# Feed-forward input product of a two-layer encoder as seven 2x2 block products

## Chip, cores, metric

The kernel runs on one core of one Trainium2 chip, in one launch. The metric is the time of an execution on the device in microseconds; the time before is the median of three runs.

## What is computed

Two encoder layers over 512 tokens of width 1024, all in float32. Each layer has a mixer (latent attention and a convolution), a cross attention to 256 memory tokens and a SwiGLU feed-forward part, each with a residual and a layer norm. The change touches the feed-forward part, with FFN_HIDDEN = 2816:

```python
def swiglu_ffn(x, w_in, w_down):
    gu = x @ w_in
    g, up = gu[..., :FFN_HIDDEN], gu[..., FFN_HIDDEN:]
    return (jax.nn.silu(g) * up) @ w_down
...
y = memory_cross_attention(x, mem, xa_w_q[l], xa_w_kv[l], xa_w_o[l])
x = layer_norm(ALPHA * x + y, ln2_g[l], ln2_b[l])
y = swiglu_ffn(x, ffn_w_in[l], ffn_w_down[l])
x = layer_norm(ALPHA * x + y, ln3_g[l], ln3_b[l])
```

## The kernel before

Every float32 operand of a matrix product is split into a rounded high part and a residue; `mm3` (L248) makes a product of three matmuls: high x high, high x residue, residue x high. ACT casts the high part, and the residue is a subtraction on DVE or Pool, or, in `added_weights` (L282), ACT writes the negated high part and an accumulating DMA from Pool's queue adds the weights from memory.

Tokens are four tiles `t` of 128. For the feed-forward input the normed x is transposed by TensorE (`transpose_x`, L426) into `xT`, eight parts of 128 features x 512 tokens, each as high part and residue. The 2816 gate and 2816 up features make 22 tiles `j` each. `ffn_blocks` (L1092) makes 44 `Block`s (L481), gate and up in turn; a block is a weight tile of 128 x 1024, fetched over SP's queue into one of three `raw` buffers, and split into one of seven `whi` and `wlo` buffers (RING); blocks from the fourth on use `added_weights`. `Block.done` runs 8 x 3 matmuls of 512 columns into one PSUM bank (`accb`, four of them; `psb` gives four more in turn). After a gate block, ACT takes tanh and DVE one operation, and after an up block DVE one more, which writes the hidden tile `hid`. Then the down projection runs over the 22 hidden tiles with weights `fdn`, and `tail` adds the residual x, which has stayed in its buffers, and norms.

Ahead of it stands the tail of the cross attention (`tail`, L513): for each token tile `second_half(t)` (L1083) makes 24 matmuls of 512 columns, and `Norm` (L457) does the residual and norm on DVE with two small Pool operations (L450, L454). The transposes of tile t-2 follow. Behind the last, `blocks[0].first`, `blocks[1].first` and `blocks[2].first` run 24 matmuls each on the first 256 tokens while tiles 2 and 3 are normed and transposed.

The order on the engines is a scheduler's, by priority and readiness, except in stretches under `issue_order` (L158): there each engine named gets its instructions in the order of the program. In the kernel before, the mixer and the start stand under it; the cross attention's tail and `ffn` do not. All engines work their queues in order. Big tiles (26 of 4 KB a partition, `bigt`) and scratch tiles (nine of 544 floats, `scr`) are shared by all stages.

## Time and profile before

| | us |
|---|---|
| runs before: median (lowest to highest) of 3 | 1485.58 (1484.5 to 1486.39) |
| the profiled execution's own time | 1483.78 |
| its span, first to last instruction | 1481.9 |
| TensorE busy in the span | 1450.8 (98%) |
| ACT busy | 721.9 (49%) |
| DVE busy | 704.1 (48%) |
| Pool busy | 469.0 (32%) |

All times of the trace are of the profiled execution, counted from its first instruction. An operation's length in the timeline includes its way through the engine's pipeline; operations that follow each other start closer together than their lengths say, so costs are read from start to start, matmuls included. A DMA's landing is counted from its issue. Layer 0's feed-forward input runs from 379 to 623 us, layer 1's from 1110 to 1354.

### The profile page before, as it was taken

The page shows a single profiled execution, that of the slowest core. Times are in us where ns is not written, and L with a number is a line of the kernel's source. Part 1 is how long each engine was busy: PE and PEld are TensorE (multiplying, and loading weights), DVE is VectorE, ACT ScalarE, POOL GpSimd, SP SyncE. Part 2 cuts the span into 40 slices and gives each one's busy share as a digit, 9 for nine tenths or more (in the row PEclk, how much of TensorE's full clock was granted, in tenths as well). Part 3 has the DMA queues.
Part 4 walks back from the last instruction along what each step waited for, and adds up shares of the span by engine and source line. Part 5 has one row for each costly group of instructions (what it writes and reads, how often), then busy time and mean ns, then how long its engine had stood idle before and what let it go on. Part 6 is the DMA issues. An engine that isn't in the chain of part 4 may idle for free.

```text
span 1481.9 us, 21183 instructions
## 1 busy us (share of the span) xinstructions
PE 1450.8 (98%) x8159; PEld 1255.3 (85%) x8159; DVE 704.1 (48%) x1187; ACT 721.9 (49%) x1278; POOL 469.0 (32%) x665
## 2 busy tenths in 40 slices
PE   8899999999999999999999999999999999999997
PEld 8799988988988888888889998888889888888886
DVE  7999677565411111310569986685662111114005
ACT  3677772452544444543146777624525444446330
POOL 2789762000211111211157987410012111111111
PEclk9999999999999999999999999999999999999999
DMA  5434343351798999999333434423419989899971
GB/s 181 149 94 150 113 157 107 100 158 56 179 212 194 197 189 194 227 195 198 113 103 122 143 122 122 157 80 105 147 57 235 194 195 197 188 194 218 197 140 57
DMA packets 64452, 227.27 MB, mean 153 GB/s; under 512 B 7328, under 2 KB 7360, under 8 KB 64352
## 3 DMA queue, kind: packets, MB, share of 16 engines
q1 hardware_dynamic: 43616, 150.75, 31.6%
q0 software_dynamic: 20736, 75.17, 28.9%
q8 instruction: 64, 1.05, 0.3%
q14 instruction: 36, 0.29, 0.1%
HBM read 213.31 MB, written 8.39 MB: 150 GB/s over the span
## 4 chain that ended last, share of the span: by engine, by line
PE 75%; DVE 10%; DMA 5%; ACT 5%; POOL 3%; issue 2%; SPq 0%; POOLq 0%; DVEq 0%; ACTq 0%
PE accb L250 19%; PE accb L251 18%; PE accb L252 18%; PE psb L250 5%; PE psb L251 5%; PE psb L252 5%; DMA raw<-in_xo 3%; DVE convb L632 2%; DVE wlo L226 2%; DVE p L862 1%; DMA raw<-in_xq 1%; ACT whi L225 1%; PE convb L250 1%; PE convb L252 1%; PE convb L251 1%
## 5 line engine op out<-in xcount | busy, mean ns | idle before, releaser
L250 PE MATMUL accb<-xTh,whi 128*128 128x512 f32 (+1 forms) x1104 | 400.0, 364 | 1.6 <-ACT whi L225 1.3
L251 PE MATMUL accb<-xTl,whi 128*128 128x512 f32 (+1 forms) x1104 | 400.7, 364 | 0.5 <-DVE xTl L436 0.4
L252 PE MATMUL accb<-xTh,wlo 128*128 128x512 f32 (+1 forms) x1104 | 399.7, 363 | 0.4 <-DVE wlo L226 0.4
L287 ACT CAST whi<-raw 128x1024 fp32r<-128x1024 f32 x126 | 132.7, 1055 | 339.4 <-PE accb L251 255.6
L250 PEld LDWEIGHTS accb<-xTh,whi 128*128 128x128 f32 x1104 | 208.3, 190 | 35.7 <-ACT xTh L433 2.7
L251 PEld LDWEIGHTS accb<-xTl,whi 128*128 128x128 f32 x1104 | 209.4, 190 | 33.2 <-DVE xTl L436 1.7
L252 PEld LDWEIGHTS accb<-xTh,wlo 128*128 128x128 f32 x1104 | 209.5, 190 | 32.5 <-DVE wlo L226 0.6
L289 POOL DMA_DIRECT2D wlo<-in_fin x82 | 71.0, 866 | 345.8 <-ACT wlo L288 336.0
L322 POOL TENSOR_TENSOR wlo<-raw,whi 128x1024 fp32r<-128x1024 f32 (+1 forms) x63 | 152.1, 2416 | 58.7 <-ACT whi L314 58.7
L1102 DVE SCALAR_TENSOR_TENSOR scr<-scr,accb 128x512 f32<-128x512 f32 x44 | 30.3, 688 | 253.3 <-ACT scr L1101 253.3
L632 DVE SCALAR_TENSOR_TENSOR convb<-ch,hvec,convb 128x511 f32<-128x511 f32 (+9 forms) x180 | 132.5, 736 | 5.6 <-ACT convb L629 1.7
L288 ACT ACTIVATE wlo<-whi 128x1024 fp32r<-128x1024 f32 x126 | 133.2, 1057 | 2.2
L226 DVE TENSOR_TENSOR wlo<-raw,whi 128x1024 fp32r<-128x1024 f32 (+1 forms) x49 | 56.6, 1158 | 128.2 <-ACT whi L225 127.4
L450 POOL TENSOR_SCALAR ve<-mv 128x1 f32<-128x1 f32 x32 | 27.5, 860 | 244.2 <-DVE mv L471 235.4
L289 POOL DMA_DIRECT2D wlo<-in_fdn x44 | 38.0, 863 | 198.4 <-ACT wlo L288 193.1
L1104 DVE SCALAR_TENSOR_TENSOR hid<-scr,accb 128x512 f32<-128x512 f32 x44 | 30.2, 687 | 136.7 <-PE accb L252 136.7
L225 ACT CAST whi<-raw 128x1024 fp32r<-128x1024 f32 (+1 forms) x49 | 48.8, 1002 | 85.9 <-PE accb L252 33.3
L623 POOL TENSOR_TENSOR cs<-cs,scr 128x511 f32<-128x511 f32 (+29 forms) x60 | 73.6, 1226 | 29.5 <-ACT scr L621 28.3
L314 ACT CAST whi<-raw 128x1024 fp32r<-128x1024 f32 (+1 forms) x63 | 66.6, 1059 | 6.0 <-PE accb L252 1.7
L250 PE MATMUL accb<-whi,hs 128*128 128x512 f32 x176 | 68.6, 389 | 0.0
L251 PE MATMUL accb<-wlo,hs 128*128 128x512 f32 x176 | 68.5, 389 | 0.0
L252 PE MATMUL accb<-whi,hs 128*128 128x512 f32 x176 | 68.5, 389 | 0.0
(297 smaller groups left out, 3160.5 us busy)
## 6 DMA issues: line engine op xcount, KB each, us to landing
raw<-in_fin SPq DMA_DIRECT2D x88, 512.0 KB, 3.6
wlo<-in_fin POOLq DMA_DIRECT2D x82, 512.0 KB, 5.9
raw<-in_fdn SPq DMA_DIRECT2D x44, 512.0 KB, 3.6
wlo<-in_fdn POOLq DMA_DIRECT2D x44, 512.0 KB, 6.1
raw<-in_xk SPq DMA_DIRECT2D x16, 512.0 KB, 3.8
raw<-in_xv SPq DMA_DIRECT2D x16, 512.0 KB, 3.6
raw<-in_wo SPq DMA_DIRECT2D x16, 512.0 KB, 3.6
raw<-in_xq SPq DMA_DIRECT2D x16, 512.0 KB, 3.6
```

Of the source, the lines that this page charges most:

```text
L225: nc.scalar.copy(hi, src)
L226: nc.vector.tensor_tensor(lo, src, hi.bitcast(F32), op=ALU.subtract)
L250: nc.tensor.matmul(o, l[0], r[0], start=first, stop=False)
L251: nc.tensor.matmul(o, l[0], r[1], start=False, stop=False)
L252: nc.tensor.matmul(o, l[1], r[0], start=False, stop=last)
L287: nc.scalar.copy(hi[:, :1024], raw[:, :1024])
L288: nc.scalar.activation(lo[:, :1024], hi[:, :1024].bitcast(F32), AF.Copy, scale=-1.0)
L289: nc.gpsimd.dma_start(out=lo[:, :1024], in_=src, accum_op=ALU.add)
L314: nc.scalar.copy(hi, raw)
L322: eng.tensor_tensor(lo, raw, hi.bitcast(F32), op=ALU.subtract)
L623: nc.gpsimd.tensor_tensor(o[:, d:], o[:, d:], part, op=ALU.add)
L632: nc.vector.scalar_tensor_tensor(out=o[:, d:], in0=src[:, :SEQ - d], scalar=tap(m, d), in1=o[:, d:], op0=ALU.mult, op1=ALU.add)
```

## The change

For each feature tile j, gate and up become the two rows of a 2x2 block matrix whose two columns are the halves of the 1024 input features; the tokens become two columns of 256 (tiles 0, 1 and tiles 2, 3). The product of 2x2 by 2x2 blocks is made with seven block products instead of eight, each of 4 x 3 matmuls of 256 columns (`Pair.product`), on seven weight blocks (gate halves "11" and "12", up half "22", sums "s1" to "s4") and seven token parts ("11", "21", "22", "t1" to "t4"), each held as high part and residue (`Halves` has the token parts, two big tiles each). Weight sums are made on DVE from the fetched tiles (`sums`, `sum4`), their high parts on ACT (`hi`), their residues on DVE (`lo`). Gate tiles and the up tile's second half are split on ACT with an accumulating DMA on Pool's queue (`added`, called by `split_gate` and `split_up`). The token differences are made on Pool (`less`), tile by tile, then transposed and split (`put`). The seven products are put together on DVE out of PSUM (`early_sums`, `late_sums`, 5 operations), then tanh on ACT and `hidden`, two operations on DVE.

The tail of the cross attention becomes `tail_pairs`: the loop over token tiles without `issue_order` (in it parts "11" and "21" are made, the gates of tiles 0 and 1 are split, and the sums of tile 0), then the token sums and the first products of tiles 0 to 2 under it. The loop over j in `ffn` stands under `issue_order` as well. The normed x no longer stays in its buffers: each tile is stored to memory (`xm`, on Pool's queue) and loaded again on SP's queue before the down projection.

```diff
+        def put(self, name, src, t):
...
+            pt = psb()
+            for k in range(4):
+                nc.tensor.transpose(pt[:, blk(k)], src[:, blk(k)], ident)
+            hi, lo = (v[:, :, blk(t % 2)] for v in self.parts[name])
+            split(pt.rearrange("p (k c) -> p k c", c=P), hi, lo)
...
+        def sums(self, x, t):
+
+            b11, b21, b12, b22 = (x[i][:, blk(h, 512)] for i in (t, t + 2) for h in range(2))
+
+            def less(a, b):
+                o = scr(name="tsum")[:, :512]
+                nc.gpsimd.tensor_tensor(o, a, b, op=ALU.subtract)
+                return o
+
+            self.put("22", b22, t)
+            yield
+            t1 = less(b12, b11)
+            self.put("t1", t1, t)
+            yield
+            t2 = less(b22, t1)
+            self.put("t2", t2, t)
+            yield
+            self.put("t4", less(b21, t2), t)
+            yield
+            self.put("t3", less(b22, b12), t)
+            yield
...
+        def added(self, hi, lo, raw, src):
+            nc.scalar.copy(hi, raw)
+            nc.scalar.activation(lo, hi.bitcast(F32), AF.Copy, scale=-1.0)
+            nc.gpsimd.dma_start(out=lo, in_=src, accum_op=ALU.add)
...
+        def product(self, o, w, xs_):
+            for k in range(4):
+                mm3(o, cut(self.ops[w], ALL, k, ALL), cut(xs_.parts[PARTNER.get(w, w)], ALL, k, ALL), k == 0, k == 3)
...
+            self.product(self.v[:, 0:256], "11", xs_)
...
+        def copy1(self):
+            self.one = scr(name="one")[:, :512]
+            nc.scalar.copy(self.one[:, 0:256], self.v[:, 0:256])
...
+            self.product(self.v[:, 0:256], "12", xs_)
...
+            self.product(self.v[:, 256:512], "s4", xs_)
...
+            self.product(self.z[:, 256:512], "s2", xs_)
+            self.product(self.z[:, 0:256], "s3", xs_)
...
+            self.product(self.z[:, 0:256], "22", xs_)
+            self.product(self.z[:, 256:512], "s1", xs_)
...
+        def early_sums(self):
+            z, h0, h1 = self.z, slice(0, 256), slice(256, 512)
+            self.u = scr(name="u")[:, :512]
+            nc.vector.tensor_tensor(self.u[:, h0], z[:, h1], self.one[:, h0], op=ALU.add)
+            nc.vector.tensor_tensor(self.u[:, h1], z[:, h0], self.u[:, h0], op=ALU.add)
+
+        def late_sums(self, dst):
+            z, u, h0, h1 = self.z, self.u, slice(0, 256), slice(256, 512)
+            nc.vector.tensor_tensor(self.one[:, h1], z[:, h1], u[:, h0], op=ALU.add)
+            nc.vector.tensor_tensor(dst.rearrange("p (a c) -> p a c", a=2), z.rearrange("p (a c) -> p a c", a=2),
+                                    u[:, h1].rearrange("p (a c) -> p a c", a=1).broadcast_to([P, 2, 256]), op=ALU.add)
+            nc.vector.tensor_tensor(self.v, self.v, self.one, op=ALU.add)
+            self.th = scr()[:, :512]
+            nc.scalar.activation(self.th, self.v, AF.Tanh, scale=0.5)
...
+    PARTNER = {"12": "21", "s4": "22", "22": "t4", "s1": "t1", "s2": "t2", "s3": "t3"}
...
+        with issue_order(tc, ORDERED):
+            early, late = xs_.sums(x, 0), xs_.sums(x, 1)
+            pairs[2].fetch_gate()
+            pairs[0].p1(xs_)
+            pairs[0].copy1()
+            pairs[0].sum4()
+            pairs[1].p1(xs_)
+            pairs[1].copy1()
+            next(early)
+            pairs[2].split_gate()
+            pairs[1].fetch_gate()
+            next(early)
+            pairs[0].p2(xs_)
+            pairs[0].split_up()
+            next(early)
+            pairs[1].fetch_up()
+            pairs[2].fetch_gate()
+            next(early)
+            pairs[1].p2(xs_)
+            next(early)
+            pairs[0].hi("s1", "s4")
+            pairs[0].lo("s1", "s4")
+            pairs[2].p1(xs_)
+            pairs[2].copy1()
+            for _ in range(2):
+                next(late)
+            pairs[2].p2(xs_)
+            for _ in range(3):
+                next(late)
...
+                if "12" in pair.ops:
+                    pair.p2(xs_)
+                if after:
+                    after.split_up()
+                if before:
+                    before.late_sums(dst(j - 1))
+                pair.p67(xs_)
+                if after:
+                    after.sums()
+                    after.hi("s3", "s2")
+                if before:
+                    before.hidden(dst(j - 1))
+                pair.early_sums()
+                if after:
+                    after.sum4()
+                    after.hi("s1")
+                    after.lo("s3", "s2")
+                pair.p3(xs_)
+                if j + 2 < NJ:
+                    pairs[j + 2].fetch_up()
+                if j + 3 < NJ:
+                    pairs[j + 3].fetch_gate()
+                if 3 <= j + 2 < NJ:
+                    pairs[j + 2].split_gate()
+                if after:
+                    after.lo("s1")
+                    if after.v is None:
+                        after.p1(xs_)
+                    after.hi("s4")
+                    after.lo("s4")
+                    if j + 1 >= 3:
+                        after.copy1()
+                pair.p45(xs_)
...
+        x = load_x(xm)
```

## Rows read from the trace of the kernel before

**Rows 1.** The page's busy time and share of the span of each engine:

```profile
PE 1450.8 (98%) x8159; PEld 1255.3 (85%) x8159; DVE 704.1 (48%) x1187; ACT 721.9 (49%) x1278; POOL 469.0 (32%) x665
```

**Rows 2.** Windows: stretch, length, each engine's busy us, PEclk, DMA share, GB/s:

```profile
379.46:623.24 243.78, 243.70 (x1153) 204.65 (x1152) 40.97 (x66) 110.15 (x132) 43.08 (x51) 1.00 0.91 203
1109.85:1353.61 243.76, 243.68 (x1154) 204.70 (x1152) 40.97 (x66) 110.13 (x132) 42.57 (x50) 1.00 0.91 203
620.00:640.00 20.00, 20.00 (x90) 16.55 (x89) 13.44 (x22) 16.86 (x27) 3.44 (x4) 1.00 0.94 223
```

**Rows 3.** Timeline, TensorE: start, length, line, out<-in, shape; matmuls 1 and 49:

```profile
479.76 0.39 PE L250 MATMUL accb<-xTh,whi 128*128 128x512 f32 x1
...
490.64 0.39 PE L250 MATMUL accb<-xTh,whi 128*128 128x512 f32 x1
```

**Rows 4.** Timeline, TensorE: eight transposes, then first and last of 66 matmuls:

```profile
379.46 0.60 PE L430 MATMUL psb<-ident,x 128*128 128x128 f32 x4
379.90 0.60 PE L430 MATMUL convb<-ident,x 128*128 128x128 f32 x4
...
382.31 0.28 PE L250 MATMUL accb<-xTh,whi 128*128 128x256 f32 x1
...
390.11 0.28 PE L252 MATMUL accb<-xTh,wlo 128*128 128x256 f32 x1
```

**Rows 5.** List of waits of TensorE: us in total, times, longest:

```profile
PE psb L553 <- DMA mem<-in_mem: 5.0, 1, 5.0
```

**Rows 6.** Timeline, DVE and ACT: runs of like operations end to end:

```profile
381.13 0.76 DVE L436 TENSOR_TENSOR xTl<-psb,xTh 128x256 fp32r<-128x256 f32 x2
...
626.35 3.71 DVE L226 TENSOR_TENSOR hs<-hid,hs 128x512 fp32r<-128x512 f32 x6 [0.78 <-ACT hs L225]
...
623.28 1.05 ACT L287 CAST whi<-raw 128x1024 fp32r<-128x1024 f32 x1
624.23 0.62 ACT L225 CAST hs<-hid 128x512 fp32r<-128x512 f32 x1
...
625.71 3.22 ACT L225 CAST hs<-hid 128x512 fp32r<-128x512 f32 x6
```

**Rows 7.** Page's groups by line, Pool: xcount | busy, mean ns | idle:

```profile
L322 POOL TENSOR_TENSOR wlo<-raw,whi 128x1024 fp32r<-128x1024 f32 (+1 forms) x63 | 152.1, 2416 | 58.7 <-ACT whi L314 58.7
...
L289 POOL DMA_DIRECT2D wlo<-in_fin x82 | 71.0, 866 | 345.8 <-ACT wlo L288 336.0
```

**Rows 8.** Timeline, DVE and Pool: norms of token tiles 2 and 3, layer 0:

```profile
375.55 1.28 DVE L475 SCALAR_TENSOR_TENSOR x<-x,mv,gb 128x1024 f32<-128x1024 f32 x1
...
384.61 1.28 DVE L477 SCALAR_TENSOR_TENSOR x<-x,rstd,gb 128x1024 f32<-128x1024 f32 x1
...
375.60 1.31 POOL L450 TENSOR_SCALAR ve<-mv 128x1 f32<-128x1 f32 x1 [4.01 <-DVE mv L471]
...
382.76 0.22 POOL L450 TENSOR_SCALAR ve<-mv 128x1 f32<-128x1 f32 x1 [1.03 <-DVE mv L471]
```

**Rows 9.** DMA issues in 377:386, 440:600, 614:634: KB, median us to landing:

```profile
wlo<-in_fin POOLq DMA_DIRECT2D x3, 512.0 KB, 9.0
...
wlo<-in_fin POOLq DMA_DIRECT2D x28, 512.0 KB, 5.7
raw<-in_fin SPq DMA_DIRECT2D x24, 512.0 KB, 3.6
...
wlo<-in_fdn POOLq DMA_DIRECT2D x4, 512.0 KB, 7.5
raw<-in_fdn SPq DMA_DIRECT2D x3, 512.0 KB, 5.8
```

**Rows 10.** Windows around TensorE's longest wait, columns as in rows 2:

```profile
49.80:54.80 5.00, 0.02 (x2) 0.02 (x1) 4.75 (x8) 3.29 (x5) 5.00 (x5) 0.74 0.73 236
54.80:59.00 4.20, 4.20 (x12) 3.52 (x13) 4.13 (x5) 1.20 (x2) 4.20 (x3) 0.50 0.50 159
59.10:63.00 3.90, 3.90 (x23) 3.38 (x22) 3.79 (x7) 2.77 (x4) 3.63 (x3) 1.00 0.47 129
```

More of the change, by code (lines that the diff above doesn't have):

```diff
@@ new lines, in encoder, with tail_pairs @@
+    PARTNER = {"12": "21", "s4": "22", "22": "t4", "s1": "t1", "s2": "t2", "s3": "t3"}
+    EARLY = 2
+    def tail_pairs(x, gb, half0, mm, pairs, keep):
+        xs_ = Halves()
+        for t in range(NT):
+            if t < EARLY:
+                pairs[t].split_gate(fetch(pairs[t].gate))
+            if t == 0:
+                pairs[0].fetch_gate()
+                pairs[0].fetch_up()
+                pairs[0].sums()
+                pairs[0].hi("s3", "s2")
+                pairs[0].lo("s3", "s2")
+            norm = Norm(x[t], gb)
+            o = mm(t)
+            for i, y in enumerate(half0(t) + o):
+                norm.half(i, y)
+            if t >= 2:
+                xs_.first(x, t - 2)
+            norm.finish(lambda rows, cols: keep(t, rows, cols))
+        with issue_order(tc, ORDERED):
[27 more added lines that the diff above has]
+                next(late)
+        return xs_
@@ L1087, in second_half, with keep, ffn @@
             return [o]
-        return tail(x, gb, lambda t: [o0[t]], second_half, nxt), nxt
+        def keep(t, rows, cols):
+            nc.gpsimd.dma_start(out=xm[blk(t), cols], in_=rows)
+        return tail_pairs(x, gb, lambda t: [o0[t]], second_half, nxt, keep), nxt
     def ffn_blocks(l):
-        return [Block(fin[l, (j % 2) * NJ + j // 2], added=j >= 3) for j in range(2 * NJ)]
-    def ffn(l, x, xT, blocks, keep):
+        return [Pair(fin[l, j], fin[l, NJ + j]) for j in range(NJ)]
+    def ffn(l, xs_, pairs, keep):
@@ L1096, in ffn, with dst @@
         last = l == DEPTH - 1
         hid = [bigt([P, 2, SEQ], F32, name="hid") for _ in range(NJ // 2)]
-        for j in range(NJ):
-            og = blocks[2 * j].done(xT)
-            th = scr()[:, :512]
-            nc.scalar.activation(th, og, AF.Tanh, scale=0.5)
-            nc.vector.scalar_tensor_tensor(out=th, in0=th, scalar=1.0, in1=og, op0=ALU.add, op1=ALU.mult)
-            ou = blocks[2 * j + 1].done(xT)
-            nc.vector.scalar_tensor_tensor(out=hid[j // 2][:, j % 2, :], in0=th, scalar=0.5, in1=ou,
-                                           op0=ALU.mult, op1=ALU.mult)
+        def dst(j):
+            return hid[j // 2][:, j % 2, :]
@@ new lines, in ffn @@
+        with issue_order(tc, ORDERED):
+            for j in range(NJ):
+                pair = pairs[j]
+                before = pairs[j - 1] if j else None
+                after = pairs[j + 1] if j + 1 < NJ else None
+                if "12" in pair.ops:
[31 more added lines that the diff above has]
+                pair.p45(xs_)
+            pairs[NJ - 1].late_sums(dst(NJ - 1))
+            pairs[NJ - 1].hidden(dst(NJ - 1))
@@ L1134, in encoder @@
     xs = dram.tile([SEQ, D], F32, name="xs")
+    xm = dram.tile([SEQ, D], F32, name="xm")
     blocks = mixer_blocks(0)
@@ L1167, in keep @@
                 nc.gpsimd.dma_start(out=xs[blk(t), cols], in_=rows)
-        xT, blocks = ffn(l, x, xT, blocks, keep)
+        xT, blocks = ffn(l, halves, pairs, keep)
 def _layout(i):
```

70 lines of the change are left out of this document (69 added, 1 removed).

## Prediction

> **What bounds the kernel now.** The page's busy times come first [rows 1]: TensorE is busy 98% of the span, so what shortens the stream of matmuls shortens the kernel. The windows then cut out the stretch the change replaces, from the last matmul of the fourth `second_half` to the end of the feed-forward input product [rows 2]: 243.78 us in layer 0 and 243.76 us in layer 1, with the granted clock at 1.00, TensorE idle 0.08 us in each, DVE busy 41 us and ACT 110 us. The list of waits says the same of the whole kernel: TensorE's longest wait, for a load of `mem`, is 5.0 us [rows 5]. So before, this stretch costs what its matmuls cost. In the timeline, matmuls of 512 columns start 10.88 us apart over 48 [rows 3], 0.2267 us each. In the first blocks, of 256 columns, 66 matmuls start from 382.31 to 390.11 [rows 4], 0.120 us each. Four transposes take 0.44 us from start to start [rows 4].
>
> **The cycle: seven products for eight.** A feature tile (gate and up) costs 2 x 8 x 3 = 48 matmuls of 512 columns now, 10.88 us; after, 7 products x 4 x 3 = 84 matmuls of 256 columns, 10.08 us at 0.120. The arithmetic falls by 12.5%, the time by 7.4%, since half the columns cost 0.120 and not 0.113. The Trainium skill (TensorE: Matmul & The Clock Gate, Back-to-back issue gap) has a matmul at its columns divided by the clock plus 2.5 ns; by that the tile would fall from 10.4 to 9.2 us, 1.2 us where the rows give 0.80, and the whole would come out 17 us below the forecast; 66 matmuls in a row at 0.120 [rows 4] leave it no chance here.
>
> Over 22 tiles, 1848 matmuls are 221.8 us. The token parts need more transposes: seven parts x two token tiles x four are 56, of which 48 now lie after the last `second_half` matmul, 5.3 us, where 24 lay. Without a wait the stretch takes 227.1 us where it took 243.8: 16.7 us less in each layer. What follows is how much of this is lost.
>
> **Other engines inside the cycle.** DVE gets, for each tile, four weight sums, four residues, two ops of 512 in the late sums, two in `hidden`, and three of 256. From start to start a 512 costs 0.604 us, a 256 from PSUM 0.33 [rows 6]: 12 x 0.604 + 3 x 0.33 = 8.2 us of 10.08. ACT gets seven passes of 512 at 0.52, two of 1024 at 0.95 [rows 6] and one of 256, at most 0.39: 5.9 us. I laid the fixed order over one period, with 0 at the end of `p45` of tile j-1. DVE: late sums to 1.8, sums of j+1 to 3.6, `hidden` to 4.8, early sums (they wait for `p67`, at 4.5) to 5.5, `sum4` to 6.1, four residues to 8.6. TensorE wants the early sums read out before `p45`, at 7.2, and the residues only in the next period. ACT splits the gate of j+2 from 5.3 to 7.2, Pool issues its residue's DMA at 7.35, and `p1` reads that residue at 10.08 + 6.0 = 16.1. It is late from a landing of 8.7 us on; landings in this stretch were 5.7, and 7.5 at its end [rows 9], where DVE was busy 67% [rows 2]. The up half of j+2 is fetched once `sum4` frees its buffer, at 6.2; with a landing of 3.6 to 5.8 [rows 9] it is there at 9.8 to 12.0, and DVE asks for it at 11.9. DMA moves 1.75 MB a tile for 2 MB. So the cycle stays bound by TensorE, at 10.08, with 1 to 2 us of slack on every side.
>
> **The head: the token sums.** Here I expect the loss. Let T be the last matmul of `second_half(3)` (379.46 in layer 0). Before, TensorE had three 256-column part blocks (2.9 us each) to cover the fourth token tile's norm, which ended 6.4 us after T [rows 8]. After, the order written out is a chain through four queues. The transposes of x[1] end at T+0.9. DVE does the residue of part 11 behind the norm's two ops, so `p1(0)` runs on from T+2.1, `p1(1)` ends at 4.9, the transposes of part 22 at 5.35. ACT copies 22 until 6.0, then splits pair 2's gate, two passes of 0.95 [rows 6], to 7.95. Pool's queue holds the accumulating DMA of that gate ahead of the first subtraction: it waits for ACT, and takes 0.86 [rows 7] to 8.9. A subtraction of 512 is half of the 1024-column Pool op at 2.40, 1.2 us [rows 7], so t1 is there at 10.1, and TensorE, which needs its transposes next, has stood since 5.35: 4.7 us. Then t1's copy, `split_up(0)` on ACT to 12.2 and its DMA on Pool to 13.1, t2 to 14.3; TensorE did `p2(0)` until 11.9 and stands another 2.3 us. t4 comes at 15.5, another 0.7. From there TensorE has work: `p2(1)`, `p1(2)`, `p2(2)` at 1.44 us each, seven sets of four transposes at 0.44 (t4 and t3 of token tile 0; 22 and four sums of tile 1), and 0.5 us for the last residue; `p67(0)` starts at T+23.3, where 48 transposes and six products are 13.9 us. Loss 9.4 us a layer. Its bounds: 5 if a subtraction takes 0.5 and the DMA's issue frees Pool early, 13 if DVE holds Pool up.
>
> That can happen: a Pool op on one column takes 1.31 us beside a DVE op of 1.28 and 0.22 otherwise [rows 8]. The Trainium skill (SBUF — State Buffer, Who interferes with whom) says that a DVE instruction with two inputs in SBUF contends with Pool's reads, which agrees with these rows; by it each of the eight subtractions could wait for one DVE op of 0.6 us, up to 5 us a layer. In the head few such ops are due, since the norm's last one ends at T+6; in the cycle they are most of DVE's, but there Pool has only DMAs to issue. So I add nothing, and leave it to the bound of 13.
>
> **The first cycles.** Tiles 0 and 1 have no `p1` of a later tile between `p3` and `p45`, since the head did it. In tile 1 DVE's late sums, sums, `hidden` and early sums (1.5 + 1.8 + 1.2 + 0.7) outlast `p67` and `p3` (4.3): 1.4 us of waiting. Gate 3 is split in tile 1, and lands about when `p1(3)` asks: 1.1 us, between 0 and 2. Sum 2.5.
>
> **The clock.** The one wait of 5.0 us was followed by 0.50 of the clock until 59.0 with the engine at work, then 1.00 again [rows 10]. A wait of 4.7 us should bring the same. The half clock falls largely on time when TensorE waits anyway; 0 to 3.4 us, I take 1.0. The Trainium skill (TensorE: Matmul & The Clock Gate, Why this matters for your kernels) tells authors to keep gaps between bursts of matmuls short for this reason.
>
> **What else moves, at nothing.** Four stores of x and four loads (2 MB each way a layer): the stores are issued on Pool before its token sums and after each norm, the loads on SP behind the last weights; if the first down-projection weights stood behind them it would cost up to 3 us a layer. The last tile's late sums and `hidden` (4 us on DVE and ACT) are hidden by the down projection, which needs that tile last. Weight sums of pair 0 in the tail (five operations of 512, 3.0 us of DVE [rows 6]) replace three residues of 1024, 3.6 us at the same rate.
>
> **Sum.** 227.1 + 9.4 + 2.5 + 1.0 = 240.0 us against 243.8: 3.8 a layer, 7.6 in all. The profiled execution has a span of 1481.9 and a time of 1483.78 (1.9 around the span); the median of the runs, 1485.58, is 1.8 above it. 1485.6 - 7.6 = 1478.
>
> **Rivals.** (1) *The head is covered.* If the subtractions run ahead of the queue or cost little, the loss falls from 9.4 to 4 us or less a layer, with no half clock: the gain is 16.7 - 4 - 2.5 = 10.2 a layer at least and 16.7 at most, 1452 to 1465. Against it: Pool's queue is written out. Chance 0.14. (2) *The residue of the gate comes late in every cycle.* The period is then its landing plus 1.35 us. It decides from a landing of 8.7; at 8.9 the gain is gone (0.2 us on each of 19 full cycles, twice); at 9.0, as where three such DMAs crowded [rows 9], the period is 10.35 and the time 0.27 x 38 = 10 us more, 1488; at 9.5 the period is 10.85, as before, and the time 1507. For it: landings grew from 5.7 to 7.5 with DVE busy, and two fetches will be in flight beside it. Against it: 1.2 us of slack, and fewer bytes. I give 1488.5 to 1507 a chance of 0.25. (3) *The small matmuls don't hold 0.120*, since each loads its own weights: 66 in a row did [rows 4]; at 0.13 there is no gain left. It is in (2)'s chance. (4) *The losses just eat the gain*: a head of 11 and an end of 2 us: 1483 to 1488, chance 0.16.
>
> **How the numbers follow.** The forecast's own case, 1465 to 1482.5, has 0.45. About 0.2%, 3 us, is what a measurement of this kernel can tell from no change. Faster by more is the forecast and (1): 0.59; within it 0.16; slower (2): 0.25. The range runs from 1464, which cuts the better half of (1), to 1496, which cuts the worse part of (2).
>
> **What would show it.** After T: TensorE waiting for transposes of a token sum, released by Pool, 4 to 5 us for the first t1, and Pool's accumulating DMA ahead of it released by ACT; a clock of 0.5 there. In the cycle: 256-column matmuls 0.120 us apart, tile to tile 10.08 us, DVE near 80% busy without TensorE waiting for it. The whole stretch near 240 us. It would be wrong if TensorE waits in every cycle (for a residue's DMA, or for DVE), if the period isn't 10.08, or if the head's `p67(0)` starts well before T+20.

## The result, and the profile after

| | us |
|---|---|
| before, median (lowest to highest) | 1485.04 (1483.69 to 1486.39) |
| after, median (lowest to highest) | 1502.74 (1502.19 to 1504.42) |
| ratio after to before | 1.0126 (95% interval 1.0114 to 1.0138) |
| span of the profiled execution, before and after | 1481.9 and 1500.9 |

The change makes the kernel 17.7 us slower; the prediction said 7.6 us faster, with a range that ended at 1496. Where the 19.0 us between the two profiled executions lie can be read from starts of matmuls in the two timelines:

| stretch | before | after | more |
|---|---|---|---|
| to the last matmul of `second_half(3)`, layer 0 | 379.2 | 382.3 | 3.0 |
| from there to the first matmul of the down projection | 244.0 | 249.3 | 5.3 |
| down projection, first to last matmul | 120.4 | 122.8 | 2.5 |
| from there to the last matmul of `second_half(3)`, layer 1 | 366.0 | 365.4 | -0.6 |
| from there to the first matmul of the down projection | 244.0 | 251.2 | 7.2 |
| down projection, first to last matmul | 119.5 | 120.9 | 1.5 |

The first and the fourth row are code that both kernels share, and 0.2 us more lie behind the last row. In layer 0's cross attention one weight of `xo` landed 1.6 us later than before, and the clock was at 0.5 for 3.4 us behind TensorE's waits that followed from it. The same stretch (from the first to the last product with `xo`) took 55.6 to 59.3 us over all kernels below, long in layer 0, in layer 1, in both or in neither, so I don't count the 2.7 of these 3.0 us that lie there as an effect of the change. The other 16.4 us (the rows are rounded) lie in the feed-forward part.

The page's busy times, which answer to [rows 1]:

```profile
PE 1433.6 (96%) x9647; PEld 1311.2 (87%) x9647; DVE 1023.4 (68%) x1749; ACT 804.7 (54%) x1500; POOL 500.9 (33%) x695
```

TensorE is busy for 17 us less in a span 19 us longer: it waits, and part of its work runs at half clock. The windows of after, with the columns of [rows 2]: the input product, the step to the down projection and the down projection's start, for layer 0 and then layer 1:

```profile
382.26:626.80 244.54, 232.38 (x1898) 230.34 (x1896) 195.68 (x338) 146.85 (x234) 55.40 (x60) 0.98 0.76 179
626.80:631.58 4.78, 0.11 (x1) 0.00 (x0) 1.65 (x4) 3.51 (x5) 1.13 (x2) 0.81 1.02 411
631.58:640.00 8.42, 8.42 (x27) 6.74 (x28) 6.17 (x10) 4.07 (x8) 1.17 (x2) 0.70 1.06 282
1119.79:1364.00 244.21, 232.12 (x1897) 230.18 (x1896) 195.60 (x338) 145.80 (x234) 54.36 (x60) 0.98 0.76 178
1364.00:1370.90 6.90, 0.36 (x4) 0.15 (x2) 1.63 (x3) 4.29 (x6) 1.08 (x2) 0.72 1.03 379
1370.90:1379.00 8.10, 8.06 (x30) 6.58 (x31) 6.19 (x10) 4.11 (x8) 0.62 (x1) 0.82 1.05 275
```

The input product now takes as long as before, 244 us: what the seven products save, its waits eat. The loss is behind it, in a step that had no wait before [rows 2, 5]. The list of waits of TensorE (total us, times, longest) names both:

```profile
PE psb L550 <- POOL tsum L564: 14.0, 4, 5.2
PE accb L250 <- ACT hs L225: 11.3, 2, 6.6
...
PE convb L250 <- DVE u L679: 2.9, 2, 1.4
```

The second line is new: TensorE waits for `hs`, the split of the first hidden tile. ACT's timeline in layer 0 shows why it is late:

```profile
624.55 1.05 ACT L287 CAST whi<-raw 128x1024 fp32r<-128x1024 f32 x1 [1.62 <-DMA raw<-in_fdn]
628.07 1.04 ACT L287 CAST whi<-raw 128x1024 fp32r<-128x1024 f32 x1 [2.47 <-DMA raw<-in_fdn]
629.02 2.00 ACT L288 ACTIVATE wlo<-whi 128x1024 fp32r<-128x1024 f32 x2
630.93 2.16 ACT L225 CAST hs<-hid 128x512 fp32r<-128x512 f32 x4
633.00 0.58 ACT L688 ACTIVATE scr<-accb 128x512 f32<-128x512 f32 x1
```

Hidden tile 0 had been ready since 423. But its split stands in ACT's queue behind the casts of the fifth and sixth down-projection weights, and these wait for their loads. The last tile's tanh (L688) stands behind it all. Before, ACT made the first split at 614.4, 9 us ahead of the end of the input product.

### The profile page after: what moved, and what is told of

The parts are those of the page before. It is cut to its first block, busy times and chain, and to the rows that moved or that the text cites. A ratio compares the mean times of both kernels' runs of the same rounds, so it can differ in the third digit from the quotient of the medians.

```text
span 1500.9 us, 25060 instructions
## 1 busy us (share of the span) xinstructions
PE 1433.6 (96%) x9647; PEld 1311.2 (87%) x9647; DVE 1023.4 (68%) x1749; ACT 804.7 (54%) x1500; POOL 500.9 (33%) x695
## 4 chain that ended last, share of the span: by engine, by line
PE 70%; DVE 10%; DMA 7%; ACT 5%; issue 4%; POOL 4%; SPq 0%; POOLq 0%; DVEq 0%; ACTq 0%
PE accb L250 12%; PE accb L251 11%; PE accb L252 11%; PE psb L250 9%; PE psb L251 9%; PE psb L252 9%; DMA raw<-in_xo 3%; PE convb L250 2%; PE convb L252 2%; PE convb L251 2%; DVE convb L844 2%; DMA raw<-in_fdn 1%; DVE wlo L226 1%; POOL tsum L564 1%; DVE p L1074 1%
## 5 line engine op out<-in xcount | busy, mean ns | idle before, releaser
L252 PE MATMUL accb<-xsh,wlo 128*128 128x256 f32 x528 | 151.7, 287 | 1.6 <-DMA wlo<-in_fin 1.6
L250 PE MATMUL accb<-xsh,whi 128*128 128x256 f32 x528 | 152.6, 289 | 0.5 <-ACT xsh L225 0.5
L251 PE MATMUL accb<-xsl,whi 128*128 128x256 f32 x528 | 151.7, 287 | 1.2 <-DVE xsl L226 1.2
L251 PE MATMUL psb<-xsl,whi 128*128 128x256 f32 x512 | 145.1, 283 | 2.7 <-DVE xsl L226 2.7
L250 PE MATMUL psb<-xsh,whi 128*128 128x256 f32 x512 | 145.1, 283 | 0.0
L252 PE MATMUL psb<-xsh,wlo 128*128 128x256 f32 x512 | 144.9, 283 | 0.0
L250 PE MATMUL accb<-xTh,whi 128*128 128x256 f32 (+1 forms) x352 | 118.4, 340 | 1.4 <-ACT whi L225 1.3
L251 PE MATMUL accb<-xTl,whi 128*128 128x256 f32 (+1 forms) x352 | 118.1, 337 | 0.4 <-DVE xTl L436 0.4
L252 PE MATMUL accb<-xTh,wlo 128*128 128x256 f32 (+1 forms) x352 | 117.7, 335 | 0.4 <-DVE wlo L226 0.4
L645 DVE TENSOR_TENSOR wlo<-ssum,whi 128x512 fp32r<-128x512 f32 x176 | 111.9, 696 | 5.2 <-ACT whi L640 5.1
```

The costliest lines, as they stand in the source:

```text
L250: nc.tensor.matmul(o, l[0], r[0], start=first, stop=False)
L251: nc.tensor.matmul(o, l[0], r[1], start=False, stop=False)
L252: nc.tensor.matmul(o, l[1], r[0], start=False, stop=last)
L645: nc.vector.tensor_tensor(lo, self.s[n], hi.bitcast(F32), op=ALU.subtract)
```

## Experiments: the step to the down projection

In the expectations and results of the runs, T is the start of the last matmul of `second_half(3)`, 0.23 us ahead of the prediction's T (382.26 and 382.50 in layer 0 of the changed kernel). The kernel before took 1483.4 to 1485.5 us in the median beside these runs; each ratio is to its own.

**x loaded late (e1).** The four loads of x (2 MB) go from the head of the down projection into its loop:

```diff
         gb = load_gb(l, 2)
-        x = load_x(xm)
...
             w, hs = operands(j)
+            if j == 6:
+                x = load_x(xm)
```

> Edit: the four loads of x for the last norm are moved from the head of the down projection into its loop, behind the operands of j = 6. Theory (queue): the changed kernel loses at the step from the input product to the down projection because the four x loads stand on SP ahead of the down-projection weights and take the first free big buffers; ScalarE's casts of two weights then wait for their loads, and the first hidden split stands behind them on ScalarE. Then the wait of TensorE for hs (4.7 us in layer 0, 6.6 us in layer 1) falls below 0.5 us in both layers, the half clock behind it goes (the down projections were 2.5 and 1.5 us longer than before the change), and the time falls by about 15 us, 1502.7 to 1487. Rival (the last tile): the down projection waits because the last tile's late sums, tanh and hidden come late or because ScalarE is full there; then moving x changes the wait by less than 1 us and the time by less than 3 us.

Measured: 1491.07 us, ratio 1.0035 (1.0018 to 1.0051). From T to the last matmul of the down projection it takes 365.8 and 366.1 us where the changed kernel takes 372.2 and 372.1, so 12.3 of the 16.4 us come back. No wait for `hs` is left; waits of 1.0 and 2.5 us remain, for the accumulator that the last input pair holds until its tanh and products are done. So the x loads are the cause, but not yet how.

**Two splits written ahead (e2).** x stays where it is:

```diff
+            first = [split_hid(0), split_hid(1)]
             pairs[NJ - 1].late_sums(dst(NJ - 1))
             pairs[NJ - 1].hidden(dst(NJ - 1))
```

> Edit: the x loads stay where the changed kernel has them; only the splits of the first two hidden tiles are written ahead, before the last tile's late sums, so that they get the first free buffers and stand on ScalarE ahead of the waiting weight casts. Theory (queue): the wait for hs goes as in the run with late x loads, since five weights are already in the ring: under 0.5 us a layer, 1487 to 1490. Rival (bandwidth): 2 MB of x, 1 MB of gain and bias and the weights crowd the DMA engines, so that the weights themselves, not the splits behind them, are late; then TensorE's wait moves to the third or later weight or its residue (3 to 6 us a layer), and the time stays above 1496.

Measured: 1501.75 us, ratio 1.0103 (1.0088 to 1.0118), so both numbers were near the rival's. The wait moved by a few matmuls, to 5.4 and 4.4 us within the first feature tile of the down projection. ACT in layer 0:

```profile
629.09 1.05 ACT L287 CAST whi<-raw 128x1024 fp32r<-128x1024 f32 x1 [0.82 <-DMA raw<-in_fdn]
632.30 1.04 ACT L287 CAST whi<-raw 128x1024 fp32r<-128x1024 f32 x1 [2.16 <-DMA raw<-in_fdn]
633.25 1.05 ACT L288 ACTIVATE wlo<-whi 128x1024 fp32r<-128x1024 f32 x1
634.21 0.58 ACT L688 ACTIVATE scr<-accb 128x512 f32<-128x512 f32 x1
```

TensorE in the same run:

```profile
635.65 0.76 PE L250 MATMUL accb<-whi,hs 128*128 128x512 f32 x1 [5.43 <-DVE scr L693]
```

It isn't a weight that TensorE waits for, as the rival had it. The last tile's tanh is what now stands behind the waiting casts; its product on DVE (L693) frees the fourth accumulator, which TensorE needs for the last token tile. The chain is the same, one member on.

**Copies for loads (e9).** Late x, and four copies of its bytes within DRAM on Pool's queue where the loads had been:

```diff
+        for t in range(NT):
+            nc.gpsimd.dma_start(out=xd[blk(t)], in_=xm[blk(t)])
```

> Edit: x is loaded late, as in the first run, but where the changed kernel loads it (behind the gains and biases) Pool's queue issues four copies of its 2 MB within DRAM, which nobody reads: as many bytes at the same time, without SP's queue and without buffers. It tells the order on SP's queue from the DMA engines' share. Theory (order on SP): the weights' loads are not behind the copies, so the time is that of the run with late loads, within 2 us, 1489 to 1493, and TensorE waits at the step to the down projection 1 to 2.5 us as there. Rival (bandwidth): the copies take the engines from the weights' loads, ScalarE's casts wait for them as in the changed kernel, and TensorE waits 3 us a layer more: 1497 or above.

Measured: 1495.53 us, ratio 1.0078 (1.0057 to 1.0098). It doesn't answer its question: nothing tied the copies to the place, and they were issued as soon as each tile of `xm` was stored, in the head (374.6 to 396.6 us in layer 0). There they cost: in layer 0 a wait of 3.1 us in the first `p1`, which is 0.6 us otherwise, since a copy waits in Pool's queue for its tile's store (up to 5.3 us) and stands ahead of the norm's operations on Pool. At the step to the down projection it did as with late loads (0.5 and 1.1 us of waits).

**Few bytes at the same place (e10).** x is loaded where the changed kernel does it, but 128 columns of 1024, the rest seven weights later:

```diff
-        x = load_x(xm)
+        x = []
+        for t in range(NT):
+            x.append(bigt([P, D], F32, name="x"))
+            nc.sync.dma_start(out=x[t][:, :128], in_=xm[blk(t), :128])
...
+                if j == 12:
+                    for t in range(NT):
+                        nc.sync.dma_start(out=x[t][:, 128:], in_=xm[blk(t), 128:])
```

> Edit: the four loads of x stay at the changed kernel's place on SP and keep their buffers, but fetch 128 of the 1024 columns there (0.25 MB for 2 MB); the other 896 follow seven weights later, long before the last norm reads them. It tells the bytes ahead of the weights from the buffers and places in the queues that x takes. Theory (bytes ahead of the weights): the wait for hs falls from 4.7 and 6.6 us to under 1.5 us a layer, 1489 to 1493. Rival (x takes the first free buffers, so that hs has none): the wait stays above 3 us a layer, above 1497.

Measured: 1491.47 us, ratio 1.0058 (1.0041 to 1.0076), a wait for `hs` of 0.7 us in one layer. This agrees with the theory of bytes, but it isn't proof of it: ACT's queue came out otherwise too, with the first four splits behind the fifth weight's cast only and no longer behind the sixth's.

**ACT's order alone (e14).** All of x at its place, with ACT's queue written out: `load_x` and the weights 0 to 5 go under the order by hand, and the splits and the tanh go ahead of the casts of weights 4 and 5:

```diff
+                    raws = [fetch(fdn[l, k]) for k in (4, 5)]
+                    first = [split_hid(0), split_hid(1)]
+                    gb = load_gb(l, 2)
+                    x = load_x(xm)
...
             pairs[NJ - 1].late_sums(dst(NJ - 1))
             pairs[NJ - 1].hidden(dst(NJ - 1))
+            first += [split_hid(2)]
+            for k, raw in zip((4, 5), raws):
+                ws.append(added_weights(fdn[l, k], raw))
+                first += [split_hid(len(first))]
```

> Edit: the changed kernel with all of x loaded at the step to the down projection, as many bytes as there and behind seven weights on SP (there six); only ScalarE's queue is written out: the splits of the first two hidden tiles and the last tile's tanh come ahead of the casts of the fifth and sixth down-projection weights, which were ahead of them. Theory (order on ScalarE): the landing of those two weights, 7 to 9 us, is the same with x and without it in the traces so far (6.8 and 8.3 us in the changed kernel, 8.6 and 9.1 us with late x loads), so what costs is that the split which TensorE needs stands behind casts that wait for them. Then the waits for hs fall to under 1 us in both layers with x's traffic unchanged: 1485 to 1491. Rival (x's bytes): the wait stays at 3 us a layer or more, or moves to a weight: above 1496.

Measured: 1486.62 us, ratio 1.0026 (1.0016 to 1.0036). From T to the end of the down projection it takes 365.6 and 364.5 us: 14.2 of the 16.4 us come back with ACT's queue in another order. TensorE waits 0.3 us for `hs` in each layer, and the down projection takes 120.8 and 119.6 us, as before the change. ACT:

```profile
623.40 1.12 ACT L225 CAST hs<-hid 128x512 fp32r<-128x512 f32 x2
626.97 0.60 ACT L688 ACTIVATE scr<-accb 128x512 f32<-128x512 f32 x1 [2.44 <-DVE accb L686]
...
632.16 1.05 ACT L287 CAST whi<-raw 128x1024 fp32r<-128x1024 f32 x1 [0.58 <-DMA raw<-in_fdn]
```

A cast still waits for its load at 632; nobody stands behind it that TensorE needs. And the loads of the two weights (issues in the stretch that has them, KB each, median us from issue to landing) are as slow with x as without. The changed kernel, 617 to 619.7:

```profile
raw<-in_fdn SPq DMA_DIRECT2D x2, 512.0 KB, 7.9
```

Late x, 616 to 619.7:

```profile
raw<-in_fdn SPq DMA_DIRECT2D x2, 512.0 KB, 9.2
```

ACT's order alone, 620 to 622.8:

```profile
raw<-in_fdn SPq DMA_DIRECT2D x2, 512.0 KB, 8.8
```

In layer 1 they took 8.9 and 10.6 us in the changed kernel, 9.2 and 10.8 with late x. So neither x's bytes nor SP's order make these two weights late; they land late here in any case, before the change too (8.3 us for the two loads issued from 613 to 619). In e14 they were issued later as well and landed 7 us later after T than in the changed kernel (T+249.0 and T+252.8 for T+242.2 and T+245.7, layer 0), and still the time came back. What the change did is to put the splits behind them. Loading x ahead of the down projection changed what the scheduler puts first on ACT; through which of its rules (the buffers that x takes, or the time it reckons for the loads) these runs don't tell.

## Experiments: the head

**The head's order (e3).** The token sums go ahead of the splits of weights:

```diff
             next(early)
-            pairs[2].split_gate()
-            pairs[1].fetch_gate()
-            next(early)
             pairs[0].p2(xs_)
-            pairs[0].split_up()
-            next(early)
-            pairs[1].fetch_up()
-            pairs[2].fetch_gate()
             next(early)
             pairs[1].p2(xs_)
             next(early)
+            next(early)
+            pairs[2].split_gate()
+            pairs[1].fetch_gate()
+            next(early)
+            pairs[0].split_up()
+            pairs[1].fetch_up()
+            pairs[2].fetch_gate()
```

(and behind it 22 and t1 of the second half ahead of `p1(2)`).

> Edit: in the head the order alone: the token sums t1, t2, t4 come ahead of the splits of pair 2's gate and pair 0's up half, so that no accumulating DMA stands before them on Pool; p2(0) stands before t1 and p2(1) before t2; the second half's 22 and t1 stand before p1(2). Theory (Pool's order): t1 is no longer behind a DMA issue that waits for ScalarE; the wait for it falls from 5.2 us to under 2, the half clock of 10.2 us in each head goes, and the first p67 starts about T+20 to T+22 where it effectively started at T+28.3: 6 to 8 us a layer, 1488 to 1491. Rival (the subtractions themselves): a subtraction takes 1.35 us on Pool and eight of them 11 us, with the norm's own Pool operations before them, so that the order is worth 3 us a layer at most: 1497 to 1500.

Measured: 1509.66 us, ratio 1.0157 (1.014 to 1.0174): slower than the changed kernel by 6.9 us, so both failed (the profiled execution, 1517.18, is the slowest of its five). The first three sums did come early (t1 needed no wait any more), but the first `p67` started at T+32.6. Pool's timeline:

```profile
391.23 1.28 POOL L564 TENSOR_TENSOR tsum<-x,tsum 128x512 f32<-128x512 f32 x1
396.18 0.93 POOL L608 DMA_DIRECT2D wlo<-in_fin  x1 [3.67 <-ACT wlo L607]
396.81 1.58 POOL L564 TENSOR_TENSOR tsum<-x 128x512 f32<-128x512 f32 x1
401.67 0.90 POOL L608 DMA_DIRECT2D wlo<-in_fin  x1 [3.27 <-ACT wlo L607]
```

The DMA issues that wait for ACT now stand between t4 and t3 and ahead of the second half's sums. Wherever they stand, the sums behind them wait, and five were behind them.

**Token sums on DVE (e5).**

```diff
-                nc.gpsimd.tensor_tensor(o, a, b, op=ALU.subtract)
+                nc.vector.tensor_tensor(o, a, b, op=ALU.subtract)
```

> Edit: the eight token subtractions go to VectorE, in the written order unchanged; Pool keeps its DMAs. VectorE does 512 columns in 0.60 us where Pool took 1.35. Theory (Pool's order): t1 then waits for neither Pool's accumulating DMA nor Pool's speed: it is there at about T+7.8 where it was at T+10.9; waits for token sums fall from 7.7 us to about 4 a layer, no half clock or half of it, the gain is 5 to 6 us a layer: 1491 to 1493. Rival (the norm of the fourth token tile is what holds t1 back, or ScalarE's splits of weights between the copies): the waits stay at 6 us or more a layer and the time falls by less than 5 us.

Measured: 1512.31 us, ratio 1.018 (1.0165 to 1.0195), 9.6 us slower than the changed kernel. t1 was there at T+8.1, about as expected, yet the first `p67` came at T+31.3. DVE:

```profile
387.39 0.68 DVE L564 TENSOR_TENSOR tsum<-x 128x512 f32<-128x512 f32 x1
389.44 0.69 DVE L226 TENSOR_TENSOR xsl<-psb,xsh 128x512 fp32r<-128x512 f32 x1 [1.37 <-ACT xsh L225]
390.05 0.68 DVE L564 TENSOR_TENSOR tsum<-x,tsum 128x512 f32<-128x512 f32 x1
```

A subtraction is twice as fast here and comes later: in the written order each stands behind the residue of the part before it, which waits for that part's transposes and ACT's copy. That is a round through three engines, 2.7 us a sum where Pool, which has no such step, takes 1.35.

**Residues on DVE (e6).** In the head, pair 2's gate and pair 0's up half get their residue from DVE:

```diff
+            if dve:
+                split(raw[:, :1024], hi[:, :1024], lo[:, :1024])
+                return
             self.added(hi[:, :1024], lo[:, :1024], raw[:, :1024], self.gate)
...
-            pairs[2].split_gate()
+            pairs[2].split_gate(dve=True)
...
-            pairs[0].split_up()
+            pairs[0].split_up(dve=True)
```

> Edit: in the head alone, the residues of pair 2's gate and pair 0's up half are formed by VectorE from the loaded weight (1024 and 512 columns, 1.2 and 0.6 us) and no longer by ScalarE's negated copy and Pool's accumulating DMA. Pool then has the token subtractions one behind the other, and the written order is otherwise that of the changed kernel. Theory (a DMA issue that waits for ScalarE blocks Pool's queue): the run with the head's order changed only moved those two blocked issues behind other subtractions, so it kept the loss; without them t1 comes at T+6.6, t2 at T+8.8, t4 at T+10.7, the second half's sums at T+13 to T+17.4, and the first p67 starts at T+18.5 to T+20 where it started at T+26.9: 7 to 9 us a layer, 1485 to 1489. Rival (the eight subtractions themselves, 1.3 us each and up to 2.2 us beside VectorE): the gain is under 3 us a layer, above 1496.

Measured: 1489.45 us, ratio 1.0038 (1.0021 to 1.0054), just outside the theory's numbers (by the traces, 12.5 us less than the changed kernel from T to the end of the down projection, both layers); the first `p67` starts at T+20.4 and T+19.4. TensorE's waits for t1, t2 and t4 are 0.85, 0.16 and 1.55 us. Pool does the sums one behind the other:

```profile
386.84 1.25 POOL L564 TENSOR_TENSOR tsum<-x 128x512 f32<-128x512 f32 x1
388.17 2.16 POOL L564 TENSOR_TENSOR tsum<-x,tsum 128x512 f32<-128x512 f32 x1
```

So what held the head up were the two DMA issues in Pool's queue that wait for ACT. (The edit also takes 1.5 us of passes off ACT, but in the changed kernel ACT itself stood idle for 3.7 us before t1's copy.) The second sum takes 0.9 us longer than the first; DVE beside it has

```profile
386.89 2.29 DVE L477 SCALAR_TENSOR_TENSOR x<-x,rstd,gb 128x1024 f32<-128x1024 f32 x1 [0.47 <-POOL rstd L454]
```

which takes 1.28 us alone [rows 8]: each costs the other a microsecond. The Trainium skill (SBUF — State Buffer, Who interferes with whom) has a DVE instruction with two inputs in SBUF contend with Pool's reads; these two lines agree. Four of layer 0's eight sums took 1.6 to 2.2 us and the others 1.3, 2.2 us more in all, so the 5 us a layer that the prediction allowed for it were too many.

**The price of the half clock (e8).** 36 transposes into a buffer that nobody reads, in the wait for t1:

```diff
+            if t == 0:
+                idle = psb()
+                for _ in range(36):
+                    nc.tensor.transpose(idle[:, 0:P], ident, ident)
             self.put("t1", t1, t)
```

> Edit: 36 transposes of the identity into a buffer that nobody reads are put ahead of the first t1's transposes in the head, into the 5.2 us in which TensorE waits there; all else as in the changed kernel. They are to keep the granted clock at 1.00 and so to price the half clock of the head by itself. Theory (the half clock lies on waits): what p2(0) loses at 0.213 us a matmul is lost again in the wait for t2, and only part of p2(1)'s loss counts: 0 to 1 us a layer, 1500.5 to 1503. Rival (the half clock adds up): p2(0) 1.1, p2(1) 1.0 and the transposes 0.3 to 0.6 us a layer come off: 1497.5 to 1498.5.

Measured: 1500.2 us, ratio 1.0111 (1.0089 to 1.0132), between the two. The interval overlaps the changed kernel's (1.0114 to 1.0138), so the time alone decides nothing, and the traces have to. In the changed kernel these stretches have the lower of the two levels, 0.50 (windows as in [rows 2]; layer 0's head, then the step behind it in either layer):

```profile
390.83:397.66 6.83, 3.68 (x16) 3.38 (x16) 0.69 (x1) 1.77 (x4) 3.22 (x4) 0.50 0.93 251
401.07:404.48 3.41, 3.41 (x18) 3.41 (x17) 0.69 (x1) 0.83 (x2) 3.25 (x4) 0.50 0.00 0
629.76:636.59 6.83, 5.01 (x12) 3.96 (x13) 4.27 (x7) 5.89 (x11) 2.30 (x3) 0.50 1.05 321
1367.04:1373.87 6.83, 2.93 (x7) 2.35 (x8) 2.19 (x4) 6.44 (x10) 1.71 (x2) 0.50 1.04 330
```

With the transposes the clock is 1.00 until past t2:

```profile
388.00:392.00 4.00, 2.71 (x22) 2.27 (x20) 0.69 (x1) 1.36 (x3) 1.86 (x2) 1.00 1.04 295
392.00:395.50 3.50, 0.58 (x5) 0.42 (x4) 0.00 (x0) 0.38 (x1) 2.74 (x3) 1.00 0.87 230
395.50:399.00 3.50, 2.81 (x15) 2.73 (x15) 1.38 (x2) 1.17 (x2) 3.42 (x4) 0.66 0.23 38
```

`p2(0)` ran 1.1 us faster, and TensorE stood 1.1 us longer for t2:

```profile
394.92 0.66 PE L550 MATMUL convb<-ident,tsum 128*128 128x128 f32 x4 [2.92 <-POOL tsum L564]
```

The changed kernel waits 1.79 us there. By the end of the head 0.5 us a layer is left of the gain, by the end of the input product 1.2, since gate 3's residue is no longer waited for. So the first stretch of half clock in the head lies on waits, as the prediction had it. The second isn't priced: here too the clock was at 0.50 from 396.6 to 400.0, under `p2(1)`. At the step to the down projection nothing covers it: there TensorE is the bound again. It was busy for 5.0 and 2.9 us of the last two stretches above, and half of that is the 2.5 and 1.5 us by which the down projection is longer.

## Experiments: what is left of the seven products

**Both mended (e7).** e1 and e6 together, and in the down projection's first feature tile the last token tile comes after the second feature tile:

```diff
-            for t in range(NT):
+            if j == 0:
+                held = w, hs
+            for t in range(NT - 1 if j == 0 else NT):
                 for half in range(2):
                     step(j, t, half, w, hs)
+                    if j == 1 and t == NT - 2 and half:
+                        for h in range(2):
+                            step(0, NT - 1, h, *held)
```

> Edit: late x loads as in the first run, the head's residues on VectorE as in the run beside this one, and in the down projection's first feature tile the last token tile's two products are done after those of the second feature tile (its accumulator is the one that the last input pair holds until its tanh and products are done). By the parts: 1491 with late x loads, 14 to 18 us less by the head, and up to 1.0 and 2.5 us less by the waits for that accumulator: 1470 to 1477, faster than before the change. If the two losses overlap or the weights' transfers bound the down projection, it stays above 1480.

Measured: 1472.45 us, ratio 0.9914 (0.9892 to 0.9936): faster than before. The parts add up: from T to the end of the down projection, both layers, e1 takes 12.3 us less than the changed kernel, e6 12.5, and e7 26.8; the 2.0 us beyond their sum are put down to the step for the accumulator, which no run shows by itself.

**Three more waits (e11)** aimed at: the first two sums ahead of the fourth norm on Pool, one order from the head into the cycles, and early sums first in tile 1:

```diff
+            if t == 2:
+                early = xs_.sums(x, 0)
+                next(early)
...
-        with issue_order(tc, ORDERED):
+        with issue_order(tc, ORDERED, xs_.chain):
...
                 pair.p67(xs_)
+                if j == 1:
+                    pair.early_sums()
                 if after:
                     after.sums()
```

> Edit on the fastest run so far: the first two token sums are written right after the third token tile's norm, ahead of the fourth's on Pool; the order by hand goes through from the head into the cycles, so that pair 1's weight sums can't pass the last token part on VectorE; in tile 1 the early sums come before the weight sums and hidden. Each aims at a wait of that run: 0.85 us for t1 and 1.55 us for t4, 1.48 us within the first p67, 1.44 us for the early sums of tile 1. If these waits are what stands between the stream of matmuls and the clock, 2.5 to 4.5 us a layer come off: 1463 to 1468. If the work only gathers at the next wait (Pool's remaining sums, VectorE), less than 1.5 us a layer: above 1469.5.

Measured: 1475.82 us, ratio 0.9949 (0.993 to 0.9967). The first `p67` came at T+18.3 for T+20.4, and the early sums' 1.44 us went, but a wait of 1.46 us for the residue of a weight sum on DVE came in their place, and a new line heads TensorE's list of waits:

```profile
PE accb L252 <- DMA wlo<-in_fin: 6.6, 2, 3.4
```

In tile 1 the weight sums now come behind the early sums, and ACT's casts of these sums with them. Gate 3's split stands behind the casts in ACT's queue:

```profile
413.91 1.67 ACT L652 CAST whi<-ssum 128x512 fp32r<-128x512 f32 x3 [3.38 <-DVE ssum L636]
415.49 1.04 ACT L612 CAST whi<-raw 128x1024 fp32r<-128x1024 f32 x1
```

Its DMA left 2.2 us later after T than in e12, and TensorE waited for it 3.4 and 3.1 us (0.9 and 1.5 in e12). (The expectation of e12 below puts this down to the buffers of the loads. The cast at 415.49 waited for no load, so it is ACT's order once more.)

**Without the step in tile 1 (e12).**

> Edit: the latest fast run without its change in tile 1, whose early sums stand again behind the weight sums: there the reordering took 1.44 us off the early sums and gave 3.4 and 1.5 us to the gate's and the up half's residues, since the weight sums free the buffers into which the next weights are loaded. Kept: the first two token sums ahead of the fourth token tile's norm on Pool, and one order by hand from the head through the cycles. By parts: the run at 1472.5 less the head's 2.1 us a layer (first p67 at T+18.3 for T+20.4) and about 1 us a layer of the wait inside that p67: 1465 to 1469.5. If the head's gain is given back later (a residue's DMA that is late in tiles 1 to 3), 1471 or more.

Measured: 1469.53 us, ratio 0.9901 (0.9886 to 0.9917), the upper end of what was expected. It is the fastest median; its interval overlaps that of e7, so which of the two is faster isn't settled. From T to the end of the down projection it takes 356.8 and 355.7 us, before 364.4 and 363.4: 7.6 and 7.8 us of the 16.7 a layer that the prediction's sum had without waits. Of the other 9, 5.6 and 6.9 are waits of TensorE that are left, the longest of them 1.8 us for the residue of a token part.

## Why the prediction was wrong, by its own steps

| a layer | predicted | measured |
|---|---|---|
| period of a cycle | 10.08 | 10.08 |
| tile 1, wait for early sums | 1.4 | 1.44 |
| gate 3's residue | 1.1 (0 to 2) | 0.85 in layer 0, 0.74 in layer 1 |
| waits for t1, t2, t4 | 4.7, 2.3, 0.7 | 5.2, 1.8, 0.7 |
| first `p67` (the prediction's T) | T+23.3 | T+26.7, and 1.3 of waiting in it |
| input product, whole stretch | 240.0 | 244.3 and 244.2 |
| wait at the step to the down projection | 0 (up to 3) | 4.7 and 6.6 |
| down projection | 0 | 2.5 and 1.5 longer |

**Right: the cycle.** DVE's early sums of tiles 3 and 19 in layer 0:

```profile
441.66 0.42 DVE L678 TENSOR_TENSOR u<-psb,one 128x256 f32<-128x256 f32 x1
...
602.94 0.42 DVE L678 TENSOR_TENSOR u<-psb,one 128x256 f32<-128x256 f32 x1
```

161.28 us in 16 cycles are 10.08 each. Matmuls of 256 columns hold 0.120 us over 84 a tile, DVE is busy 86% from 420 to 600 (80% predicted), TensorE waits for nothing from 436 to 620, and the gate's residue lands in 6.6 us in the median, short of the 8.7 from which rival 2 decides:

```profile
wlo<-in_fin POOLq DMA_DIRECT2D x44, 512.0 KB, 6.6
```

So rival 2, whose 1488.5 to 1507 holds the measured time, has the number by chance: its mechanism didn't occur. Rival 3 is out by the same lines.

**Right in kind, short in size: the head.** TensorE's waits in layer 0:

```profile
393.42 1.12 PE L550 MATMUL psb<-ident,tsum 128*128 128x128 f32 x4 [5.21 <-POOL tsum L564]
...
398.89 0.66 PE L550 MATMUL psb<-ident,tsum 128*128 128x128 f32 x4 [1.79 <-POOL tsum L564]
400.23 0.66 PE L550 MATMUL convb<-ident,tsum 128*128 128x128 f32 x4 [0.69 <-POOL tsum L564]
...
410.88 0.39 PE L251 MATMUL psb<-xsl,whi 128*128 128x256 f32 x1 [1.34 <-DVE xsl L226]
```

Each wait is where the prediction put it and nearly as long; e6 shows that the cause is the one it named, DMA issues that wait for ACT in Pool's queue. What was missed lies between the waits: t1 came 0.8 us later than reckoned, t2 2.1 (t1's transposes ran at half clock, and ACT ended its passes for `split_up` at T+13.8 for T+12.2, by the prediction's T), `p2(1)` took 0.9 more at half clock, and the last residue cost 1.3 for 0.5, since pair 1's weight sums got ahead of it on DVE. The loss is 14.1 us where 9.4 and 1.0 for the clock were taken; that is inside the sum of their upper bounds, 13 and 3.4 (for the 3.4 the prediction shows no row). With the cycles as predicted, these 3.7 us are nearly all that makes 244.3 of 240.0, no gain and no loss: by the head alone it would be the case of rival 4, 1483 to 1488.

**The step that failed: "What else moves, at nothing".** Two of its sentences. It let the four loads of x cost up to 3 us if the first weights stood behind them on SP. They didn't stand behind them: six weights were issued ahead of x, and the last two of these landed as late without x at that place (e1) as with it. What moved was the order on ACT, in which the splits of the hidden tiles came to stand behind two weight casts; I asked which transfer is late, not which queue waits for it and what is queued behind. And it called the last tile's late sums and `hidden` hidden, since the down projection needs that tile last. The tile, yes; but its pair holds one of four accumulators, and the down projection needs all four in its first feature tile. In the changed kernel itself the wait for `hs` hides this; it comes out where that wait goes (e2: 5.4 and 4.4 us; e1: 1.0 and 2.5). Both sentences priced one resource and left out the queue. With them goes the clock: 4.7 and 6.6 us of waiting left the clock at 0.5 for 6.8 us, where the prediction counted the clock only in the head. The waits and the clock behind them are 15.2 of the 16.4 us (11.25 and 3.95), and e14, which takes them away, gets back 14.2.

The range failed with this step: its only cases for a loss behind the stretch were an end of 2 us in rival 4 and the 3 us that were not taken into the sum, for 7.2 and 8.1 a layer measured, and its slower side hung on the cycle alone.

## What to carry to other kernels

A transfer that is slow costs nothing until something needed stands behind the instruction that waits for it: for each engine that works in order, list what is queued behind every wait on a DMA, and put what the next stage needs ahead of it (14 us here, by the order of one queue). An edit that only moves loads can change that order on an engine it doesn't touch, so the first few instructions of the next stage belong into the sum, with the buffers and accumulators that the last ones hold. A saving in arithmetic is worth its stream only if the edges hold: of 16.7 us a layer, the head took 14 and the step behind it 7 to 8, and once both were mended nearly half of it was had.

## What the runs showed of the hardware

- TensorE's clock fell behind waits of 1.7 and 0.9 us too, not only behind waits near 5 us [rows 10]. In layer 0's cross attention in the changed kernel it was at the lower level from 332.8 to 336.2, with TensorE at work throughout (columns as in [rows 2]):

```profile
332.80:336.20 3.40, 3.40 (x18) 3.40 (x18) 2.52 (x4) 0.78 (x2) 0.00 (x0) 0.50 0.48 148
```

- Loads of 512 KB on SP that landed in 3.4 to 3.5 us a few microseconds earlier (the first three down-projection weights of the changed kernel, layer 0) took 7 to 11 us at the step to the down projection, and those issued behind x 20 to 25 us, without TensorE waiting for these.
- Pool's subtraction of 512 columns costs 1.2 to 1.4 us from start to start; the prediction's 1.2, half of a 1024-column operation, was near.
